# Scan of a bidirectional gated recurrence: filler weights' low parts by negative copy and accumulating DMA, one update per level for keys and queries, first decays copied by ScalarE

## The chip, the cores and the metric

The kernel runs on one core of a Trainium2 chip. The metric is the device time of one launch in microseconds (us), as the median of several runs. A profiled execution beside them gives the span from the first to the last instruction, and the records that are quoted below.

## What is computed

One layer of an encoder on a sequence of 1024 positions with 1024 channels, in float32. The part that this change is about is the two-way recurrence of one of its two token mixers, for 8 heads of 128 channels, in each direction:

```python
h = rmsnorm(x)
proj = h @ w_in                      # q, v, z_f, z_b, output gate, merge gates, ...
f = lb + (1 - lb) * sigmoid(z)       # decay per position and channel
k = (1 - lb) * sigmoid(-z)
S_t = diag(f_t) S_{t-1} + k_t v_t^T  # state, 128 x 128 per head
o_t = S_t^T q_t                      # forward and backward scan, added
```

The other mixer is a gated depthwise convolution. Both are merged by gates (sigmoid of the last columns of the projection), projected, and followed by a gated feed-forward part and a last norm.

## The kernel before

**Matmuls in float32.** A weight tile is split into a high part, rounded to the format that TensorE multiplies fast (fp32r), and a low part, the rest. `split` (L123) does so: ScalarE copies the raw page to the high part, and VectorE subtracts the high part from the raw page to get the low one. `mm3` (L147 to L149) then makes three matmuls per 128 rows: high weights with high inputs, high weights with low inputs, low weights with high inputs. The third is the first to read a low part.

**Jobs.** The projection's columns are computed 128 at a time by jobs (`std_job`). A job's `prep` loads the raw weights (`raw_w`, L134, 512 KB on SyncE's queue, two pages "wr") and splits them into two pages of four ("wp"). Its `run` issues 8 steps of six matmuls: 4 steps for each half of the sequence, each half ending with an `evac` that copies the result from the bank to a page "ev" (L720, L722) and stores it in DRAM. `run_jobs` prepares the next job when a job starts. `duo_job` runs two jobs, half by half.

**The scan stage.** After the convolution's pointwise jobs (tile "ch", pages of 512 elements), 22 columns of the projection are left, merge gates that nobody needs yet: 20 standard jobs and one `duo_job`. They are the stream `dense`, filler for TensorE while the scan runs. `dense.fill(1.3)` issues one step, sometimes two. The stream starts with `dense.fill(21)`, ahead of the first scan level.

The scan walks over 16 half-heads (8 heads, 2 halves of 512 positions). For each one:

- `scan_inputs` loads q and the gates' inputs z of both directions (L1060, L1063) and lets ScalarE compute the keys (k) and decays (f) from them.
- `scan_base` (L1078 on) builds products of decays inside blocks of 8 positions in the tile DE, a reciprocal, and from them the scaled queries Qh, qF and keys Kh, kG. It is a generator: the base of the next half-head is advanced by two steps at a time between the levels of the present one. `tt` (L1042) is its product on VectorE, `keys` (L1045) a scaled product.
- `scan_levels` takes four levels, with blocks of h = 8, 16, 32 and 64 positions. At h = 8 and 16 ScalarE copies the keys into a page A (L1160), and 16 small matmuls multiply A with the queries (L1162; bank "sc" at 8, bank "ob" at 16). At 32 and 64 the matmuls read keys and queries directly (L1188). Then one VectorE product each updates the keys (kG) and the queries (qF) by the blocks' decays tb, for the next level, and a small one merges tb.
- `scan_states` transposes the keys (L1245), copies them, multiplies them with the values (L1254) and chains the states on VectorE (Sf, L1260 and L1262; Sb, L1347).
- `scan_outputs`, spread over the next half-head, multiplies states and scores (L1295), normalises (a power on GpSimd, L509 and L510, and scaling on ScalarE, L1314), and transposes (L1321).

Between these steps `between(FILL)` issues filler steps, two base steps and one step of the pending outputs.

**Order.** TensorE's instructions run in the order in which the program issues them (`manual_schedule`). The other engines' order is laid out ahead of time by the framework's scheduler from the dependencies; every engine then runs its own list strictly in order, and waits on semaphores.

**DMA.** SyncE issues the ordinary ones. GpSimd issues those that add to their target (`accum_op`); before, only the pair jobs of other stages use them (L300).

Of the kernel before, what the change touches and what calls it, by code (L numbers as in the profile page):

```python
# [10 lines left out]
F32 = mybir.dt.float32  # L11
# [35 lines left out]
def tile_hybrid_encoder(  # L47
# [45 lines left out]
    def nm(s):  # L93
        uid[0] += 1
        return f"{s}_{uid[0]}"
# [6 lines left out]
    def page(pool, tag, bufs, dt=F32):  # L102
        return pool.tile([P, H], dt, tag=tag, name=nm(tag), bufs=bufs)
# [395 lines left out]
    def in_cols(c0):  # L499
        return w_cols(w_in, 0, ND, c0)  # L500
# [576 lines left out]
    def scan_base(ins):  # L1077


        q, f, kk, ks = ins  # L1080

        def two(t, *r):
            if len(r) == 1:
                return view(t, r[0], [[8, N2]])
            return view(t, r[0], [[r[1] - r[0], 2], [8, N2]])

        fv = lambda *r: two(f, *r)
        ed = lambda *r: two(DE, *r)
        D = D0


        V.tensor_copy(ed(2, D + 4), fv(3, 4))
# [24 lines left out]
        along = [[8, NB], [1, 8]]  # L1117
        for d in range(2):
            m0, st = ((0, 1), (7, -1))[d]
            whole = [[8, NB], [st, 8]]  # L1120
            tt(view(Qh, (1 - d) * H + m0, whole), view(q, m0, whole), view(DE, D + d * H, along))
            yield
            keys(
                view(Kh, d * H + m0, whole),
                view(kk, d * H + m0, whole),
                ks[:, d : d + 1],
                view(DE, d * H, along),
            )
            yield
        both = [[H, 2], [8, NB], [1, 8]]  # L1130
        tt(view(qF, 0, both), view(Qh, 0, both), view(fm, 0, [[NB, 2], [1, NB], [0, 8]]))
        yield
        tt(view(kG, 0, both), view(Kh, 0, both), view(DE, D + 7, [[H, 2], [8, NB], [0, 8]]))
        yield
        yield qF, kG, [(Qh[:, 1 - d, :], Kh[:, d, :]) for d in range(2)], tb

    def scan_levels(base, S_t, Tt):


        qF, kG, qk, tb = base  # L1140
# [16 lines left out]
        def level(b, h):  # L1157

            A_t = page(hp, "A", 2)
            A.copy(A_t.rearrange("p (b x e) -> p b x e", x=2, e=h), pairs(kG, h))  # L1160
            for at, g, o in each():
                T.matmul(  # L1162
                    b[g, o].rearrange("p (b x e) -> p b x e", x=2, e=h),
                    A_t[:, at : at + 32],
                    view(qF, at, [[2 * h, 16 // h], [H + h, 2], [1, h]]),
                    start=True,
                    stop=True,
                )
# [13 lines left out]
        def blocks(b, h):  # L1182

            for c in range(0, H, P):
                for s0 in range(0, P, h):
                    t0 = s0 ^ h
                    d = s0 // h % 2
                    T.matmul(  # L1188
                        b[s0 : s0 + h, c + t0 : c + t0 + h],
                        kG[:, d, c + s0 : c + s0 + h],  # L1190
                        qF[:, 1 - d, c + t0 : c + t0 + h],
                        start=True,
                        stop=True,
                    )
# [7 lines left out]
        for h in (8, 16, 32, 64):  # L1202
# [5 lines left out]
            else:  # L1208
# [1 line left out]
                    b = bank("sc")  # L1210
                    T.matmul(b, none[:, :P], none, start=True, stop=True)
                blocks(b, h)
            tt(pairs(kG, h), pairs(kG, h), view(tb, 1, [[2, n], [nb - 1, 2], [0, h]]))
            tt(pairs(qF, h), pairs(qF, h), view(tb, nb + 1, [[2, n], [nb - 1, 2], [0, h]]))
            if h < 64:
                tn = hp.tile([P, 3, NB], F32, tag="tb", name=nm("tb"), bufs=3)
                k = 3
# [17 lines left out]
                    A.copy(S_t[g : g + 32, :, g : g + 32], D_t[g : g + 32])  # L1235
            yield

    def scan_states(i, kG, v, Tt, Sf, Sb):

        half = i % 2  # L1240
        kTs = []
        for d in range(2):
            b = bank("tr")
            for c in range(4):
                T.transpose(b[:, c * P : (c + 1) * P], kG[:, d, c * P : (c + 1) * P], ident)  # L1245
            kT = page(hp, "kT", 2)
            A.copy(kT, b)
            kTs.append(kT)
            yield
# [27 lines left out]
    def scan_outputs(h, kept, Sf, Sb):  # L1277
# [3 lines left out]
        ss = cp.tile([P, 2, 4], F32, name=nm("oss"), tag="oss", bufs=2)  # L1281
        rs = cp.tile([P, 2, 4], F32, name=nm("ors"), tag="ors", bufs=2)
        for half in range(2):
            S_t, v, qF = kept[half]
            o = bank("ob")
            for c in range(4):
                sl = slice(c * P, (c + 1) * P)
                g = half * 4 + c
                terms = [(S_t[:, c, :], v[:, c, :])]
                if g > 0:  # L1290
                    terms.append((qF[:, 1, sl], Sf[half][:, c, :]))
                if g < 7:
                    terms.append((qF[:, 0, sl], Sb[half][:, c, :]))
                for n, (l, r) in enumerate(terms):
                    T.matmul(o[:, sl], l, r, start=(n == 0), stop=(n == len(terms) - 1))  # L1295
# [73 lines left out]
    for h in range(NH):  # L1369
# [4 lines left out]
        for half in range(2):  # L1374
# [13 lines left out]
            for n, _ in enumerate(scan_levels(base, S_t, Tt[:, half])):  # L1388
# [7 lines left out]
            qF, kG = base[0], base[1]  # L1396
            for _ in scan_states(i, kG, v, Tt, Sf, Sb):
                between(FILL)
            kept.append((S_t, v, qF))
            cur = ahead  # L1400
        pending = Stream(outputs(h, kept, Tt, Sf, Sb))

# [397 lines left out]
```

## Time and profile before

| what | value |
|---|---|
| median of 3 runs | 1792.36 us (1791.06 to 1793.42) |
| span of the profiled execution | 1788.8 us |
| granted TensorE clock, mean | 0.996 |
| TensorE matmul busy | 1733.0 us (97%) |
| TensorE weight load busy | 1416.7 us (79%) |
| VectorE busy | 1250.4 us (70%) |
| ScalarE busy | 775.0 us (43%) |
| GpSimd busy | 153.8 us (9%) |
| DMA, over the span | 155 GB/s, of queue q0 (GpSimd's) 32.51 MB |

The profile names engines PE (matmul), PEld (weight load), DVE (VectorE), ACT (ScalarE), POOL (GpSimd) and SP (SyncE). A group row gives the source line, engine, operation, output<-inputs by tile name, the shape, the count, and behind the bar the busy time, the mean duration in ns, and the idle time of the engine before them with what ended it. A wait row reads "who <- whom: us in total, times, longest". The scan stage is the stretch from 500 to 906 us. Matmuls are pipelined, so PE's busy time holds a little slack; its idle time is real.

### The profile page before, as it was taken

What the parts mean: (1) busy time and instruction counts of PE and PEld (TensorE: products, weight loads), DVE (VectorE), ACT (ScalarE), POOL (GpSimd) and SP (SyncE); (2) the same over time, 40 slices, a digit from 0 to 9 for tenths busy, and PEclk for the clock granted to TensorE, in tenths of its full rate; (3) what the DMA queues carried; (4) which work ended last, traced back from release to release, by engine and by line L of the source; (5) the groups of instructions that cost most, each with busy time, mean ns of one, the idle gap of its engine ahead of it and who ended that gap; (6) DMA issues with size and microseconds to landing.
All of it is one profiled execution on the core that took longest, in us unless ns stands there. A gap on an engine that the chain in (4) does not pass through costs nothing.

```text
span 1788.8 us, 27583 instructions
## 1 busy us (share of the span) xinstructions
PE 1733.0 (97%) x10632; PEld 1416.7 (79%) x10638; DVE 1250.4 (70%) x1884; ACT 775.0 (43%) x1490; POOL 153.8 (9%) x168
## 2 busy tenths in 40 slices
PE   8989999999999999999999999999999999999997
PEld 6878877888777777777778888878888888888885
DVE  5599999746569999999645557667667667544455
ACT  7344333334555566655442245344344344422123
POOL 2201111000000000000000002011111111000000
PEclk9999999999999999999999999999999999999999
DMA  8657887743663433333257665567667665534233
GB/s 285 216 151 187 185 185 185 199 150 126 199 214 101 125 119 119 119 119 101 90 180 219 200 201 177 153 142 159 151 144 158 142 151 133 161 103 126 79 91 135
DMA packets 317705, 276.41 MB, mean 155 GB/s; under 512 B 14462, under 2 KB 242566, under 8 KB 317574
## 3 DMA queue, kind: packets, MB, share of 16 engines
q1 hardware_dynamic: 276406, 242.15, 43.1%
q0 software_dynamic: 41168, 32.51, 12.6%
q8 instruction: 83, 1.36, 0.3%
q14 instruction: 48, 0.39, 0.1%
HBM read 185.73 MB, written 72.61 MB: 144 GB/s over the span
## 4 chain that ended last, share of the span: by engine, by line
PE 65%; DVE 19%; DMA 5%; issue 4%; ACT 4%; POOL 1%; SPq 0%; POOLq 0%; DVEq 0%; ACTq 0%
PE mm L147 16%; PE mm L148 16%; PE mm L149 16%; PE sc L147 3%; PE sc L149 3%; PE sc L148 3%; DVE acc L955 2%; DVE kG L1042 2%; DVE DE L1042 2%; DVE qF L1042 2%; DVE wp L123 2%; PE tr L147 1%; PE tr L149 1%; PE tr L148 1%; DVE DE L1098 1%
## 5 line engine op out<-in xcount | busy, mean ns | idle before, releaser
L147 PE MATMUL mm<-hx,wp 128*128 128x512 f32 x1128 | 454.8, 403 | 9.8 <-DVE ev L717 4.3
L149 PE MATMUL mm<-hx,wp 128*128 128x512 f32 x1128 | 441.7, 392 | 1.9 <-DVE wp L123 1.9
L148 PE MATMUL mm<-hx,wp 128*128 128x512 f32 x1128 | 441.4, 391 | 0.0
L123 ACT CAST wp<-wr 128x1024 fp32r<-128x1024 f32 (+2 forms) x179 | 167.0, 934 | 359.6 <-PE mm L148 271.5
L147 PEld LDWEIGHTS mm<-hx,wp 128*128 128x128 f32 x1128 | 212.5, 188 | 55.7 <-DVE ev L717 6.7
L123 DVE TENSOR_TENSOR wp<-wr,wp 128x1024 fp32r<-128x1024 f32 (+2 forms) x177 | 191.4, 1082 | 90.4 <-ACT wp L123 90.1
L149 PEld LDWEIGHTS mm<-hx,wp 128*128 128x128 f32 x1128 | 212.6, 188 | 49.3 <-DVE wp L123 3.2
L148 PEld LDWEIGHTS mm<-hx,wp 128*128 128x128 f32 x1128 | 212.9, 189 | 40.4 <-issue 0.2
L955 DVE SCALAR_TENSOR_TENSOR acc<-gl,v_b,acc 128x1024 f32<-128x1024 f32 x120 | 149.0, 1277 | 0.5
L1651 DVE TENSOR_TENSOR xr<-mm,xr 128x512 f32<-128x512 f32 x48 | 33.2, 691 | 73.1 <-PE mm L149 73.1
L367 ACT COPY su<-mm 128x512 f32<-128x512 f32 x78 | 45.2, 579 | 62.5 <-PE mm L149 61.5
L123 ACT CAST wq<-sw 128x1024 fp32r<-128x1024 f32 x39 | 41.0, 1051 | 64.4 <-issue 28.6
L1500 DVE SCALAR_TENSOR_TENSOR tm<-gp,v_a,tm 128x512 f32<-128x512 f32 x88 | 65.9, 749 | 2.0
L147 PE MATMUL mm<-hy,wp 128*128 128x512 f32 x156 | 61.5, 394 | 1.4 <-ACT su L367 1.4
L148 PE MATMUL mm<-hy,wp 128*128 128x512 f32 x156 | 61.1, 392 | 0.0
L147 PE MATMUL sc<-hy,wq 128*128 128x512 f32 x156 | 61.1, 392 | 0.0
L149 PE MATMUL sc<-hy,wq 128*128 128x512 f32 x156 | 61.1, 391 | 0.0
L147 PE MATMUL tr<-hx,wp 128*128 128x512 f32 x156 | 60.8, 390 | 0.0
L149 PE MATMUL tr<-hx,wp 128*128 128x512 f32 x156 | 60.7, 389 | 0.0
L148 PE MATMUL tr<-hx,wp 128*128 128x512 f32 x156 | 60.7, 389 | 0.0
L148 PE MATMUL sc<-hy,wq 128*128 128x512 f32 x156 | 60.7, 389 | 0.0
L149 PE MATMUL mm<-hy,wp 128*128 128x512 f32 x156 | 60.6, 389 | 0.0
(368 smaller groups left out, 3467.6 us busy)
## 6 DMA issues: line engine op xcount, KB each, us to landing
wr<-in_w_in_dram SPq DMA_DIRECT2D x56, 512.0 KB, 4.7
wr<-in_ffn_w_up_dram SPq DMA_DIRECT2D x24, 512.0 KB, 4.9
sw<-in_ffn_w_up_dram SPq DMA_DIRECT2D x44, 256.0 KB, 3.0
d_g<-ft SPq DMA_DIRECT2D x44, 256.0 KB, 2.7
sw<-in_ffn_w_up_dram POOLq DMA_DIRECT2D x20, 512.0 KB, 8.3
sw<-in_w_in_dram SPq DMA_DIRECT2D x34, 256.0 KB, 3.2
d_z<-ev SPq DMA_DIRECT2D x32, 256.0 KB, 3.1
zi<-d_z SPq DMA_DIRECT2D x32, 256.0 KB, 3.2
```

The lines of the kernel that those rows point to most:

```text
L123: parts = A.copy(hi, src), eng.tensor_tensor(lo, src, hi.bitcast(F32), op=ALU.subtract)
L147: T.matmul(acc, whi[:, k, :], ahi, start=first, stop=False, skip_group_check=again)
L148: T.matmul(acc, whi[:, k, :], alo, start=False, stop=False, skip_group_check=again)
L149: T.matmul(acc, wlo[:, k, :], ahi, start=False, stop=last, skip_group_check=again)
L367: A.copy(t, acc)
L955: V.scalar_tensor_tensor(acc, g[:, k : k + S], tap(k), acc, op0=ALU.mult, op1=ALU.add)
L1042: V.tensor_tensor(o, a, b, op=op)
L1098: V.reciprocal(ed(D, 7), ed(0, D + 7))
L1500: V.scalar_tensor_tensor(c, g[:, o + k : o + k + H], vec("fdw", k * NF + j), c, op0=ALU.mult, op1=ALU.add,)
L1651: V.tensor_tensor(xr[i][half], acc, xr[i][half], op=ALU.add)
```

## The change

1. **Filler weights.** The 20 standard jobs of `dense` become `dma_job`s. The high part is copied by ScalarE as before. The low part is now a second ScalarE copy, the high part times -1, onto which GpSimd's DMA adds the raw weights from DRAM. VectorE has no part in it. `fetch` loads the raw page of the next job one job ahead. The `duo_job` at the end stays as it was.
2. **One update per level.** kG and qF become planes of one tile KQ (planes 0 and 2 keys, 1 and 3 queries, three buffers), and the two products per level become one of 1024 elements per partition.
3. **First decays.** The copy into DE (L1092) goes from VectorE to ScalarE.
4. The pages for z go from three to two.

```diff
+    def dma_job(src, nk, acts, evac, fetch, after):
+        def prep():
+            raw = fetch(src)
+            if after is not None:
+                fetch(after)
+            hi, lo = w_page(nk), w_page(nk)
+            A.copy(hi, raw)
+            A.activation(lo, hi.bitcast(F32), AF.Copy, scale=-1.0)
+            G.dma_start(lo, src, accum_op=ALU.add)
+            return hi, lo
+
+        return prep, std_job(None, nk, acts, evac)[1]
...
-    rest_jobs = [std_job(in_cols(c), ND, h_std, e) for c, e in rest[:-2]]
+    srcs = [in_cols(c) for c, _ in rest[:-2]]
+    rest_jobs = [
+        dma_job(src, ND, h_std, e, fetch, after)
+        for src, (_, e), after in zip(srcs, rest, srcs[1:] + [None])
+    ]
...
-            z = page(hp, "zi", 3)
+            z = page(hp, "zi", 2)
...
-        V.tensor_copy(ed(2, D + 4), fv(3, 4))
+        A.copy(ed(2, D + 4), fv(3, 4))
...
-        qF = hp.tile([P, 2, H], F32, tag="qF", name=nm("qF"), bufs=3)
-        kG = hp.tile([P, 2, H], F32, tag="kG", name=nm("kG"), bufs=2)
+        KQ = hp.tile([P, 4, H], F32, tag="KQ", name=nm("KQ"), bufs=3)
...
-        def pairs(t, h):
-            return view(t, 0, [[2 * h, H // (2 * h)], [H + h, 2], [1, h]])
+        def pairs(h, n):
+            return view(KQ, 0, [[2 * h, n], [2 * H + h, 2], [1, h]])
...
-            A.copy(A_t.rearrange("p (b x e) -> p b x e", x=2, e=h), pairs(kG, h))
+            A.copy(A_t.rearrange("p (b x e) -> p b x e", x=2, e=h), pairs(h, H // (2 * h)))
...
-            tt(pairs(kG, h), pairs(kG, h), view(tb, 1, [[2, n], [nb - 1, 2], [0, h]]))
-            tt(pairs(qF, h), pairs(qF, h), view(tb, nb + 1, [[2, n], [nb - 1, 2], [0, h]]))
+            tt(pairs(h, nb), pairs(h, nb), view(tb, 1, [[2, nb], [nb - 1, 2], [0, h]]))
```

The other edits only read keys and queries from their planes of KQ.

More of the change, by code (lines that the diff above doesn't have):

```diff
@@ L1016, in tile_hybrid_encoder, with fetch @@
     rest = todo[2 * NPAIRS :]
-    rest_jobs = [std_job(in_cols(c), ND, h_std, e) for c, e in rest[:-2]]
+    fetched = {}
+    def fetch(src):
+        at = src.offset
+        if at not in fetched:
+            fetched[at] = raw_w(src, ND)
+        return fetched[at]
+    srcs = [in_cols(c) for c, _ in rest[:-2]]
[3 more added lines that the diff above has]
+    ]
     (c0, e0), (c1, e1) = rest[-2:]
@@ L1129, in scan_base @@
             yield
-        both = [[H, 2], [8, NB], [1, 8]]
-        tt(view(qF, 0, both), view(Qh, 0, both), view(fm, 0, [[NB, 2], [1, NB], [0, 8]]))
+        both, apart = [[H, 2], [8, NB], [1, 8]], [[2 * H, 2], [8, NB], [1, 8]]
+        tt(view(KQ, H, apart), view(Qh, 0, both), view(fm, 0, [[NB, 2], [1, NB], [0, 8]]))
         yield
-        tt(view(kG, 0, both), view(Kh, 0, both), view(DE, D + 7, [[H, 2], [8, NB], [0, 8]]))
+        tt(view(KQ, 0, apart), view(Kh, 0, both), view(DE, D + 7, [[H, 2], [8, NB], [0, 8]]))
         yield
-        yield qF, kG, [(Qh[:, 1 - d, :], Kh[:, d, :]) for d in range(2)], tb
+        yield KQ, [(Qh[:, 1 - d, :], Kh[:, d, :]) for d in range(2)], tb
     def scan_levels(base, S_t, Tt):
-        qF, kG, qk, tb = base
-        def pairs(t, h):
-            return view(t, 0, [[2 * h, H // (2 * h)], [H + h, 2], [1, h]])
+        KQ, qk, tb = base
+        def pairs(h, n):
+            return view(KQ, 0, [[2 * h, n], [2 * H + h, 2], [1, h]])
         def near(t):
@@ L1164, in level @@
                     A_t[:, at : at + 32],
-                    view(qF, at, [[2 * h, 16 // h], [H + h, 2], [1, h]]),
+                    view(KQ, H + at, [[2 * h, 16 // h], [2 * H + h, 2], [1, h]]),
                     start=True,
@@ L1189, in blocks @@
                         b[s0 : s0 + h, c + t0 : c + t0 + h],
-                        kG[:, d, c + s0 : c + s0 + h],
-                        qF[:, 1 - d, c + t0 : c + t0 + h],
+                        KQ[:, 2 * d, c + s0 : c + s0 + h],
+                        KQ[:, 3 - 2 * d, c + t0 : c + t0 + h],
                         start=True,
@@ L1236, in scan_levels, with scan_states @@
             yield
-    def scan_states(i, kG, v, Tt, Sf, Sb):
+    def scan_states(i, KQ, v, Tt, Sf, Sb):
         half = i % 2
@@ L1244, in scan_states @@
             for c in range(4):
[L1245 removed]
+                T.transpose(b[:, c * P : (c + 1) * P], KQ[:, 2 * d, c * P : (c + 1) * P], ident)
             kT = page(hp, "kT", 2)
@@ L1283, in scan_outputs @@
         for half in range(2):
-            S_t, v, qF = kept[half]
+            S_t, v, KQ = kept[half]
             o = bank("ob")
@@ L1290, in scan_outputs @@
                 if g > 0:
-                    terms.append((qF[:, 1, sl], Sf[half][:, c, :]))
+                    terms.append((KQ[:, 3, sl], Sf[half][:, c, :]))
                 if g < 7:
-                    terms.append((qF[:, 0, sl], Sb[half][:, c, :]))
+                    terms.append((KQ[:, 1, sl], Sb[half][:, c, :]))
                 for n, (l, r) in enumerate(terms):
@@ L1395, in tile_hybrid_encoder @@
                 between(FILL)
-            qF, kG = base[0], base[1]
-            for _ in scan_states(i, kG, v, Tt, Sf, Sb):
+            KQ = base[0]
+            for _ in scan_states(i, KQ, v, Tt, Sf, Sb):
                 between(FILL)
-            kept.append((S_t, v, qF))
+            kept.append((S_t, v, KQ))
             cur = ahead
```

## The prediction, made before the changed kernel was run

> **What bounds the kernel now.** I began with the engines' busy time by window, because the change touches one stage alone: the scan with its dense filler jobs, 500 to 906 us on the profile's axis.
>
> ```profile
> 600.00:700.00 100.00, 94.48 (x1243) 77.23 (x1245) 92.70 (x193) 57.13 (x141) 4.48 (x4) 1.00 0.39 123
> ...
> 500.00:906.00 406.00, 384.88 (x4694) 315.42 (x4698) 346.20 (x700) 230.75 (x560) 14.44 (x17) 1.00 0.37 118
> ```
>
> The columns are the window and its length, then busy time of TensorE, its weight load, VectorE, ScalarE and GpSimd, the granted clock, the DMA share and GB/s. In the middle TensorE works 94.5% of the time and VectorE 92.7%. So both are nearly full, the clock is whole, and all that can be won here is TensorE's idle time: 406.0 - 384.9 = 21.1 us, 1.2% of the span. The waits of TensorE in this window tell what that idle time is.
>
> ```profile
> PE ob L1162 <- DVE qF L1042: 6.0, 7, 1.5
> PE tr L1245 <- DVE kG L1042: 4.9, 7, 1.8
> PE sc L1188 <- DVE qF L1042: 3.8, 7, 1.2
> PE ob L1295 <- DVE Sb L1347: 1.4, 1, 1.4
> PE ob L1295 <- DVE D L1230: 1.1, 1, 1.1
> ```
>
> Each row gives the total, the number of waits and the longest. They add to 17.2 us, all on VectorE, mostly on the per-level updates of keys (kG) and queries (qF). The change's target is thus the right one. Whether it hits depends on two things: how late an update starts, and how long the chain is from one level's matmuls to the next's.
>
> **What leaves VectorE.**
>
> ```profile
> L1042 DVE TENSOR_TENSOR qF<-qF,tb 128x512 f32<-128x512 f32 x64 | 43.8, 684 | 0.4 <-PE sc L1162 0.4
> L1042 DVE TENSOR_TENSOR kG<-kG,tb 128x512 f32<-128x512 f32 x64 | 43.6, 682 | 3.5 <-PE sc L1188 2.9 <-ACT A L1160 0.4
> ...
> L123 DVE TENSOR_TENSOR wp<-wr,wp 128x1024 fp32r<-128x1024 f32 x22 | 26.9, 1222 | 12.7 <-ACT wp L123 12.7
> ...
> L1042 DVE TENSOR_TENSOR kG<-Kh,DE 128x1024 f32<-128x1024 f32 x16 | 19.5, 1219 | 0.1
> ...
> L1092 DVE COPY DE<-f 128x256 f32<-128x256 f32 x16 | 6.7, 418 | 0.0
> ```
>
> Twenty subtractions for low parts at 1.222 us: 24.4 us. Sixty-four pairs of 512 elements become one of 1024: 0.684 + 0.682 - 1.219 (the price of the x16 row with 1024 elements) = 0.147 us each, 9.4 us. Sixteen copies at 0.418: 6.7 us. Together 40.5 us of 346, so VectorE falls from 92% to some 82% in the middle.
>
> **What goes to ScalarE** is twenty negative copies of 1024 elements and sixteen copies of 256.
>
> ```profile
> L123 ACT CAST wp<-wr 128x1024 fp32r<-128x1024 f32 x21 | 21.9, 1044 | 18.2 <-PE mm L148 16.0 <-DMA wr<-in_w_in_dram 2.1
> ...
> L1160 ACT COPY A<-kG 128x512 f32<-128x512 f32 x32 | 19.7, 616 | 20.9 <-DVE kG L1042 20.8
> ```
>
> 20 x 1.044 = 20.9 us, and 16 x 0.4 (between nothing and the 0.616 of 512 elements; nearest VectorE's own 0.418) = 6.4 us. ScalarE goes from 231 to 258 of 406 us, 64%; it does not become a bound, and I price its load at nothing beside the chain below. The first decays are read only after the reciprocal and several products behind it on VectorE, which cover the copy.
>
> **The accumulating DMA.** No 512 KB accumulation runs in this stage before, but 31 run elsewhere.
>
> ```profile
> sw<-in_ffn_w_up_dram POOLq DMA_DIRECT2D x20, 512.0 KB, 8.3
> ...
> sw<-in_w_in_dram POOLq DMA_DIRECT2D x11, 512.0 KB, 8.8
> ```
>
> The last number is the median from issue to landing. A single one, issued at 1164.7, is the fast end:
>
> ```profile
> sw<-in_ffn_w_up_dram POOLq DMA_DIRECT2D x1, 512.0 KB, 6.6
> ```
>
> So a low part is there 1.04 + 8.3 = 9.3 us after its high part, where the subtraction took 1.22. In the steady stage that is hidden. Preparation of job n+1 starts with job n, and the high parts tell how far apart jobs are:
>
> ```profile
> L123 ACT CAST wp<-wr x18: 1032/1044/1053, 537.7 to 882.2; 128x1024 fp32r<-128x1024 f32 x18
> ```
>
> (882.2 - 537.7) / 17 = 20.3 us, against 1.04 + 1.04 + 8.3 = 10.4: some 10 us to spare. Extra traffic (10.5 MB) meets a DMA share of 0.37. GpSimd was busy 14.4 us; behind a waiting issue stands only the output scale's power, which is needed some steps later. Two pages for the gates' inputs instead of three still leave a whole half-head between a page's last reader and its next load. All of this I take as nothing.
>
> **The first job is not hidden.** It is prepared while the last pointwise job runs. Its page comes free only then, so its work starts 3.3 us before TensorE reads the low part:
>
> ```profile
> 497.75 1.05 ACT L123 CAST wp<-wr 128x1024 fp32r<-128x1024 f32 x1 [1.68 <-PE mm L148]
> ```
> ```profile
> 500.80 0.53 POOL L1036 MEMSET none<- 128x512 bf16 x1 [0.76 <-PE mm L149]
> 500.80 0.39 PE L148 MATMUL mm<-hx,wp 128*128 128x512 f32 x1
> ...
> 501.03 0.40 PE L149 MATMUL mm<-hx,wp 128*128 128x512 f32 x1
> ```
>
> Columns: start, duration, engine. The third matmul (L149, 501.03) reads the low part. Afterwards the negative copy can run from 498.80 to 499.84. The DMA is issued then, or at about 501.4 if GpSimd's queue has the memsets first. It lands at 499.8 + 6.6 = 506.4 at the earliest, at 501.4 + 8.8 = 510.2 at the latest. TensorE's order is written by hand, so nothing else fills: it stands for 5.4 to 9.2 us. I take 499.8 + 8.3 = 508.1, **+7 us**. The second job is prepared during the first and has the stall besides; the third has one job of 48 matmuls, 0.23 us from one start to the next (500.80 to 501.03), some 11 us, against 10.4: nothing, at most 2 us.
>
> The Trainium skill, "DMA: Bandwidth & Descriptors", section "Anatomy of one DMA — SWDGE (gpsimd) path", fits a GpSimd-issued DMA as 2.0 us plus bytes over 436 GB/s; for 512 KB that is an estimate of 3.2 us, and the first job's stall by it would be 2 us. The 31 accumulations of this trace took 8.3 and 8.8 us in the median, so I go by them.
>
> **The chain from level 8 to level 16 grows.** Until now the keys' update waits only for ScalarE's copy A of the keys, and can run a level ahead of TensorE. The merged one also writes the queries, so it waits for the level's matmuls. Behind it come the next copy A, and then the next matmuls. Beside it TensorE has one filler step of six matmuls, sometimes two. Two passages, the second with transposes besides:
>
> ```profile
> 758.40 0.45 PE L1162 MATMUL sc<-qF,A 128*32 128x32 f32 x30
> ...
> 759.19 1.22 DVE L123 TENSOR_TENSOR wp<-wr,wp 128x1024 fp32r<-128x1024 f32 x1
> ...
> 761.16 0.46 PE L1162 MATMUL ob<-qF,A 128*32 128x32 f32 x32 [0.74 <-DVE qF L1042]
> ```
> ```profile
> 643.14 0.45 PE L1162 MATMUL sc<-qF,A 128*32 128x32 f32 x30
> ...
> 644.07 0.68 DVE L1042 TENSOR_TENSOR kG<-kG,tb 128x512 f32<-128x512 f32 x1
> ...
> 645.55 0.46 PE L1162 MATMUL ob<-qF,A 128*32 128x32 f32 x32
> ```
>
> In the first, level 8 ends at 758.85 and TensorE is back at 761.16 - 0.74 = 760.42. Without the subtraction VectorE could start at 759.2: + 1.22 + 0.62 (copy A) + 0.1 for hand-overs = 761.1, idle 0.7 us as before. In the second, VectorE is free at 644.07: + 1.94 = 646.0, where nothing was lost: +0.45. Per half-head I take +0.3 (between 0, if each update starts at once, and 0.75, if it starts 0.6 us later still), 16 times: **+5 us** (0 to +12). From level 16 on, an update of 1.22 stands where two of 0.68 stood back to back, or, at the transposes, where 0.68 alone did.
>
> **Relief elsewhere.** The other VectorE waits are 4.9 + 3.8 + 1.4 + 1.1 = 11.2 us. They come from VectorE's queue, which loses a tenth of its work, but the transposes' link grows by 0.54. I take half gone, **-5 us** (-11 to +2); the first passage's waits fall in the first job's stall and are counted here.
>
> **Sum:** 7 + 5 - 5 = +7 us. The profiled execution has a span of 1788.8 us and the median of the runs is 1792.36, 3.6 above, for what lies around it. The span becomes 1795.8, the time **1799.4 us**, +0.4%. A difference of 0.2%, 3.6 us, is about what a measurement tells from none.
>
> **Rivals.**
> - *The relief wins (faster).* The place is level 16. If the scheduler, with a lighter VectorE queue, starts each merged update as its matmuls end, the chain is 1.94 us against a cover of 1.57 (760.42 - 758.85) and 1.96 (645.55 - 643.59): some 0.3 us, 5 us in all, and the other 11 us go. The stage's idle is then near 9; with 5.4 for the first job 14.4, against 21.1: -7, **1785 us**. It turns at an idle of 14 us beside the first job's stall. For it: 17.2 of 21 us wait for VectorE. Against: in both passages VectorE was in other work when the level ended. Chance 0.22.
> - *The low parts come late in many jobs (much slower).* ScalarE is in order; it waits 16.0 us for pages in the row above, and the negative copy, GpSimd's issue and the landing follow in series. If half of twenty jobs lose 1.5 us more, +15: **1814 us**. Against: 10 us to spare. Chance 0.13.
> - *It washes out.* The first job's stall gives VectorE a lead that lasts, the stall is near 5.4 and the level chain costs nothing net: +5.4 - 5 = 0, **1792 us**. Chance 0.13.
>
> The forecast has 0.52, its own range 1796 to 1806. Eight in ten: 1785 (half of the first rival below) to 1812 (most of the second above). Faster by over 0.2%: 0.22; within: 0.13; slower: 0.52 + 0.13 = 0.65.
>
> **What would show it.** Right: an idle of 5 to 9 us of TensorE before the first filler job's third matmul, released by the accumulating DMA; a larger sum for ob L1162, now released by ScalarE's copy A; less for L1188 and L1295; VectorE near 306 us in the stage; no DMA wait in later jobs. Wrong: no stall at the first job (the DMA lands in under 2 us, or is issued earlier), or ob L1162 under 6 us, which means the merged updates start at once; and a wait for low parts in many jobs, which means the spare 10 us were not there.

## The result, and the profile after

| what | before | after |
|---|---|---|
| median | 1792.89 us (1791.06 to 1794.90, 4 runs) | 1821.13 us (1820.34 to 1822.68, 4 runs) |
| span of the profiled execution | 1788.8 us | 1820.9 us |
| granted TensorE clock, mean | 0.996 | 0.988 |

The ratio is 1.0152, with a 95% interval of 1.0134 to 1.017: slower, by 28 us where the forecast had 7, and above the top of the range, 1812. The direction came out, the size did not.

The place was the foreseen one. Each filler job has 48 matmuls in both kernels, so the first matmul of the same job can be set side by side in the two traces: job 0 starts 3.2 us later than before, job 1 15.4 later, job 2 15.4, and the matmuls behind the last job 31.5 later; at the end of the span it is 32.1. The 3.2 us arise ahead of the change, where both kernels have the same instructions. Two things are left: 12.2 us at the first job, and some 16 spread over the rest of the scan.

The windows of the changed kernel, in the columns of the prediction's first fence:

```profile
600.00:700.00 100.00, 93.24 (x1159) 76.03 (x1158) 78.47 (x150) 62.87 (x153) 10.13 (x8) 0.98 0.51 129
...
500.00:906.00 406.00, 369.39 (x4391) 299.96 (x4391) 305.81 (x577) 250.84 (x565) 45.98 (x38) 0.97 0.57 139
```

VectorE was relieved as planned, from 92.7 to 78.5 us in the middle hundred; a part of that fall is that less of the scan lies in these hundred. For TensorE put 1159 matmuls through them instead of 1243, and its clock is no longer whole. TensorE's waits in the stage, which now lasts to 945 us:

```profile
PE ob L1188 <- ACT A L1186: 17.0, 13, 3.3
PE mm L149 <- DMA wp<-in_w_in_dram: 10.2, 2, 9.3
PE tr L1270 <- DVE KQ L1069: 2.8, 7, 0.7
PE tr L1346 <- ACT tm L1339: 2.1, 1, 2.1
PE sc L1279 <- ACT kT L1272: 1.5, 3, 0.9
PE sc L1188 <- ACT A L1186: 1.5, 2, 1.2
PE ob L1320 <- DVE Sb L1372: 1.4, 1, 1.4
PE sc L1214 <- DVE KQ L1069: 1.3, 1, 1.3
```

Lines have moved: L1188 is the level matmul of blocks 8 and 16 (L1162 before), L1186 the copy A, L1214 the blocks of 32 and 64 (L1188 before), L1270 the key transposes, L1069 the product, L1119 the copy of the first decays. Two rows are new at the top, 17.0 us ahead of level 16 and 10.2 us for low parts (9.3 in the first job, 0.9 in the third). The row of the transposes fell from 4.9 to 2.8 and that of the blocks from 3.8 to 1.3.

**The first job**, in the timeline (start, duration, engine, and in brackets the idle time and its releaser):

```profile
502.47 1.06 ACT L276 ACTIVATE wp<-wp 128x1024 fp32r<-128x1024 f32 x1
...
503.83 1.62 POOL L277 DMA_DIRECT2D wp<-in_w_in_dram  x1 [44.74 <-PE mm L148]
```
```profile
513.66 0.79 PE L149 MATMUL mm<-hx,wp 128*128 128x512 f32 x1 [9.26 <-DMA wp<-in_w_in_dram]
514.25 0.63 PE L147 MATMUL mm<-hx,wp 128*128 128x512 f32 x1
514.68 0.63 PE L148 MATMUL mm<-hx,wp 128*128 128x512 f32 x1
```

The negative copy ends at 503.53, the DMA is issued at 503.83, and the matmul that reads the low part starts at 513.66. TensorE stood for 9.26 us. Then the matmuls come 0.43 us apart (514.25 to 514.68) instead of 0.23. The windows of this stretch show why, and what the DMAs did meanwhile (the last three columns are the granted clock, the DMA share and GB/s):

```profile
503.00:514.00 11.00, 1.74 (x8) 1.13 (x7) 0.00 (x0) 4.93 (x6) 4.36 (x6) 0.78 1.07 257
```
```profile
513.00:520.00 7.00, 6.34 (x16) 4.99 (x17) 1.34 (x2) 3.08 (x5) 0.00 (x0) 0.54 1.24 257
```

Half the clock is granted until 519.4 us; 13 matmuls at 0.20 us too much are 2.6 us. Stall and slow clock are 12 us together. The landing, in the rows of DMA issues (KB, median us to landing), first of all twenty and then of this one alone:

```profile
wp<-in_w_in_dram POOLq DMA_DIRECT2D x20, 512.0 KB, 8.4
```
```profile
wp<-in_w_in_dram POOLq DMA_DIRECT2D x1, 512.0 KB, 9.8
```

The median came as priced, 8.3. This first one took 9.8, in a stretch where the DMA engines are full (share 1.07, against 0.57 over the stage): the loads of the scan's first inputs run with it.

**A passage from level 8 to level 16.** VectorE, ScalarE and TensorE in one timeline of the changed kernel:

```profile
784.40 1.74 DVE L1125 RECIPROCAL DE<-DE 128x256 f32<-128x256 f32 x1
...
785.42 0.45 PE L1188 MATMUL sc<-KQ,A 128*32 128x32 f32 x30
...
786.82 1.20 DVE L1069 TENSOR_TENSOR KQ<-KQ,tb 128x1024 f32<-128x1024 f32 x1
...
788.05 0.62 ACT L1186 COPY A<-KQ 128x512 f32<-128x512 f32 x1 [0.69 <-DVE KQ L1069]
...
788.72 0.46 PE L1188 MATMUL ob<-KQ,A 128*32 128x32 f32 x32 [1.29 <-ACT A L1186]
```

Level 8 ends at 785.87. VectorE is inside the next half-head's reciprocal until 786.14, then does three small products, and starts the merged update at 786.82. Copy A follows it, and TensorE, which had six filler matmuls, waits 1.29 us. The update's own chain (1.20 + 0.03 + 0.62 + 0.05 = 1.90 us) is the predicted one; the 0.95 us ahead of it come from what stands in VectorE's queue. The reciprocal had not been there: in the trace of before it never lies between the end of level 8 or 16 and the queries' update, in 32 passages. In the changed kernel it lies there 10 times (8 behind level 8, 2 behind level 16). That was the surprise, and the third theory below.

### The profile page after: what moved, and what is told of

It reads as the page before. It is cut to its first block, busy times and chain, and to the rows that moved or that the text cites. A ratio compares the mean times of both kernels' runs of the same rounds, so it can differ in the third digit from the quotient of the medians.

```text
span 1820.9 us, 27583 instructions
## 1 busy us (share of the span) xinstructions
PE 1746.3 (96%) x10638; PEld 1423.2 (78%) x10638; DVE 1221.0 (67%) x1784; ACT 804.6 (44%) x1526; POOL 185.8 (10%) x188
## 4 chain that ended last, share of the span: by engine, by line
PE 45%; DMA 3%; DVE 3%; issue 2%; ACT 2%; POOL 1%; SPq 0%; POOLq 0%; ACTq 0%; DVEq 0%
PE mm L147 12%; PE mm L148 12%; PE mm L149 12%; PE sc L149 2%; PE sc L147 2%; PE sc L148 2%; DMA sw<-in_ffn_w_up_dram 2%; DMA wr<-wr 1%; PE tr L147 1%; PE tr L148 1%; PE tr L149 1%; PE ob L1320 1%; DVE KQ L1069 1%; DMA wr<-sw 0%; DVE Sb L1372 0%
## 5 line engine op out<-in xcount | busy, mean ns | idle before, releaser
L149 PE MATMUL mm<-hx,wp 128*128 128x512 f32 x1128 | 445.5, 395 | 11.6 <-DMA wp<-in_w_in_dram 10.2
L123 ACT CAST wp<-wr 128x1024 fp32r<-128x1024 f32 (+2 forms) x159 | 146.2, 920 | 357.0 <-PE mm L148 257.0
L123 DVE TENSOR_TENSOR wp<-wr,wp 128x1024 fp32r<-128x1024 f32 (+2 forms) x157 | 168.0, 1070 | 89.9 <-ACT wp L123 89.6
L1069 DVE TENSOR_TENSOR KQ<-KQ,tb 128x1024 f32<-128x1024 f32 x64 | 77.9, 1217 | 9.7 <-PE sc L1188 6.1
L315 POOL DMA_DIRECT2D wr<-sw x31 | 27.7, 894 | 375.7 <-DVE wp L123 232.5
L147 PE MATMUL mm<-hy,wp 128*128 128x512 f32 x156 | 61.6, 395 | 2.1 <-ACT su L382 2.1
L148 PE MATMUL mm<-hy,wp 128*128 128x512 f32 x156 | 61.1, 392 | 0.0
L147 PE MATMUL sc<-hy,wq 128*128 128x512 f32 x156 | 61.1, 392 | 0.0
L149 PE MATMUL sc<-hy,wq 128*128 128x512 f32 x156 | 61.0, 391 | 0.0
```

Source lines behind the costliest of these rows:

```text
L123: parts = A.copy(hi, src), eng.tensor_tensor(lo, src, hi.bitcast(F32), op=ALU.subtract)
L147: T.matmul(acc, whi[:, k, :], ahi, start=first, stop=False, skip_group_check=again)
L148: T.matmul(acc, whi[:, k, :], alo, start=False, stop=False, skip_group_check=again)
L149: T.matmul(acc, wlo[:, k, :], ahi, start=False, stop=last, skip_group_check=again)
L315: G.dma_start(o, a, accum_op=ALU.add)
L1069: V.tensor_tensor(o, a, b, op=op)
```

## The experiments

Three theories for the 28 us: **(1)** the first filler job's low part comes late; **(2)** the merged update lengthens the way from level 8 to 16; **(3)** the copy of the first decays on ScalarE, priced at nothing, costs by what it does to VectorE's order. The rival to (1) was the prediction's, low parts late in many jobs; the rival to (2) that the shared tile, not the merging, costs; the rival to (3) that the copy costs as load on ScalarE. All ratios are to the kernel before, run beside each experiment, with 95% intervals; 0.2% is 3.6 us.

### Each part alone

**The accumulating DMA alone** (dma_only): before, with `dma_job` and `fetch` as in the change.

```diff
-    rest_jobs = [std_job(in_cols(c), ND, h_std, e) for c, e in rest[:-2]]
+    rest_jobs = [dma_job(src, ND, h_std, e, fetch, after) for ...]
```

> Only the filler weights' low parts change; updates of keys and queries stay two per level, and the first decays stay on VectorE. Theory: the first job's 12 us minus some relief for VectorE: 1798 to 1806 us, with no DMA wait after the second job. Rival (the accumulating DMAs cost throughout): 1815 us or more.

Measured: 1803.31 us beside 1795.93, ratio 1.0047 (1.003 to 1.0064). TensorE waits 11.1 us for low parts, in the first and the third job only (10.3 and 0.8), and job 1 starts 14 us late; up to 4 us of that come back later. The prediction's rival of low parts late in many jobs has no wait to show, here or in the changed kernel.

**The merged update alone** (merge_only): before, with KQ and one product per level, two z pages, the decays' copy left on VectorE.

```diff
-            tt(pairs(kG, h), pairs(kG, h), view(tb, 1, [[2, n], [nb - 1, 2], [0, h]]))
-            tt(pairs(qF, h), pairs(qF, h), view(tb, nb + 1, [[2, n], [nb - 1, 2], [0, h]]))
+            tt(pairs(h, nb), pairs(h, nb), view(tb, 1, [[2, nb], [nb - 1, 2], [0, h]]))
```

> Only the merged update (tile KQ, two pages for z); low parts and first decays stay on VectorE. Theory: the copy A for level 16 now waits for level 8's matmuls, so TensorE waits there about 17 us in all against 6.8: 1800 to 1810 us. Rival (one instruction instead of two is what relieves VectorE, the waits at level 16 come from elsewhere): 1793 us or less.

Measured: 1805.67 beside 1795.93, 1.005 (1.0032 to 1.0067). The two largest waits of TensorE in it:

```profile
PE ob L1176 <- ACT A L1174: 13.4, 10, 1.8
PE tr L1258 <- DVE KQ L1057: 7.5, 7, 2.3
```

Against 6.0 and 4.9 before, that is 10.0 us more, but other rows fell: all of TensorE's waits in the stage together rose by 6 us, and the time by 9.7. The rest fits the granted clock, which is half in four stretches of 3.4 us of this scan and whole in the scan of before. In 10 passages of 16 the update and the copy behind it outlast TensorE's filler; and the keys for the transposes, now in the same product as the queries, come later.

**The decays' copy alone** (decays_only): before, with one line changed.

```diff
-        V.tensor_copy(ed(2, D + 4), fv(3, 4))
+        A.copy(ed(2, D + 4), fv(3, 4))
```

> Only the first decays are copied by ScalarE. Theory: VectorE's products into DE wait for that copy in its queue (9.4 us of such waits in the changed kernel's profile), so it gives no gain and may cost: ratio 1.000 to 1.004, with DE waiting for ScalarE's DE. Rival (16 copies off VectorE are a relief): ratio 0.996 to 0.999.

Measured: 1808.60 beside 1794.66, 1.0091 (1.0076 to 1.0106). Both theories had this too small: the line that moves 6.7 us of work off VectorE is the costliest single part, +14 us by the medians and 16 by the ratio. It isn't a direct wait: VectorE waits for the copy once, 0.3 us. First TensorE's waits in this kernel, then a stretch of VectorE with the matmuls behind it:

```profile
PE ob L1162 <- DVE qF L1042: 12.5, 10, 3.0
PE sc L1188 <- DVE qF L1042: 5.5, 8, 1.4
PE sc L1162 <- ACT A L1160: 4.7, 5, 2.1
```
```profile
752.24 0.46 PE L1162 MATMUL ob<-qF,A 128*32 128x32 f32 x32
...
752.93 1.74 DVE L1098 RECIPROCAL DE<-DE 128x256 f32<-128x256 f32 x1
...
755.16 0.67 DVE L1042 TENSOR_TENSOR qF<-qF,tb 128x512 f32<-128x512 f32 x1
...
755.88 0.46 PE L1188 MATMUL sc<-qF,kG 128*32 128x32 f32 x32 [1.36 <-DVE qF L1042]
```

Level 16 ends at 752.70, and the queries' update, 0.67 us long, starts 2.46 us later, because the next half-head's reciprocal stands ahead of it in VectorE's list. It lies so in 8 of the 32 passages (4 behind level 8, 4 behind level 16). From the end of a level to the next level's matmuls TensorE idles 11.8 us in these 8 passages and 7.4 in the other 24; before, it was 8.9 in all 32.

### Parts taken out of the changed kernel

**The first filler job prepared as before** (first_std):

```diff
+    rest_jobs[0] = std_job(srcs[0], ND, h_std, rest[0][1])
```

> Theory: the changed kernel's 28 us are (a) the first filler job's wait for its low part, 9.3 us idle and about 2.6 us of half-clock matmuls behind it, (b) the longer chain from level 8 to level 16, some 10 us of TensorE waits, and (c) half-clock stretches that these pauses bring on. With the first filler job prepared by VectorE as before, (a) goes: about 1809 us (1805 to 1812). Rival: accumulating DMAs and their traffic slow the whole stage, and the first wait is made up later anyway: 1816 us or more.

Measured: 1819.03 beside 1795.93, 1.0124 (1.0099 to 1.0149). A miss: the wait went to the second job (4.3 us, one wait) and level 16 rose to 19.2 us, with the reciprocal in the way 11 times. One job as cover isn't enough, since the second job's page is prepared in the same stretch.

**The same, with two products per level in the KQ tile** (two_updates):

```diff
-            tt(pairs(h, nb), pairs(h, nb), view(tb, 1, [[2, nb], [nb - 1, 2], [0, h]]))
+            tt(part(0, h, n), part(0, h, n), view(tb, 1, [[2, n], [nb - 1, 2], [0, h]]))
+            tt(part(H, h, n), part(H, h, n), view(tb, nb + 1, [[2, n], [nb - 1, 2], [0, h]]))
```

> The changed kernel with the first filler job prepared by VectorE and with two updates per level, keys and then queries, in the one tile KQ. Theory: both known costs go and VectorE's relief is left: 1785 to 1795 us, TensorE's wait at level 16 at or under 7 us. Rival (the accumulating DMAs cost throughout): as with the merged update and the same first job, within 3 us of it.

Measured: 1810.51 beside 1795.93, 1.0087 (1.0065 to 1.0109). Without the merge, and with the first job covered, it is still 15 us above the kernel before; level 16 waits 12.2 us, and the reciprocal is in the way 10 times. What was left of the change here was the decays' copy and the second job's wait; this miss led to decays_only.

**The decays' copy given back to VectorE** (undo_decays): the changed kernel, with one line the other way.

```diff
-        A.copy(ed(2, D + 4), fv(3, 4))
+        V.tensor_copy(ed(2, D + 4), fv(3, 4))
```

> The changed kernel with the first decays copied by VectorE again. Theory: VectorE's waits for ScalarE's copy delay the merged updates (up to 3 us late at level 16 in three passages); without them the wait at level 16 falls from 17 to about 13 us, as with the merged update alone, and the time to 1814 to 1818 us. Rival (ScalarE's load by negative copies makes copy A late): no change, 1820 to 1823 us.

Measured: 1811.02 beside 1794.66, 1.0102 (1.0086 to 1.0119), some 9 us less than the changed kernel and below the 1814 to 1818 us of the theory. Level 16 waits 9.7 us instead of 17.0, and the reciprocal is in the way in no passage. A second thing goes with the copy here. In the changed kernel VectorE did wait for it, ahead of the reciprocal:

```profile
DVE DE L1069 <- ACT DE L1119: 9.4, 7, 3.6
```

This is the base's second product, DE<-f,DE. It reads and writes other columns of DE than the copy does, and still it waits.

**The accumulating DMA from the fourth job on** (dma_from_fourth): dma_only, with three standard jobs first.

```diff
+    rest_jobs[:3] = [
+        std_job(s, ND, h_std, e) for s, (_, e) in zip(srcs[:3], rest)
+    ]
```

> The accumulating DMA alone, from the fourth filler job on; the first three are prepared by VectorE, updates and first decays are as before the change. Theory: the DMA's only price is the first job's wait and its half clock; from there on it relieved VectorE (dma_only gained about 5 us between the first and the last level 8): 4 to 6 us under the kernel before, ratio 0.997 to 0.998, no DMA wait of TensorE. Rival (that relief came from VectorE's lead during the first wait, not from the DMA): ratio 0.999 to 1.002.

Measured: 1790.48 beside 1794.66, 0.9977 (0.9966 to 0.9988). This is faster than both kernels. TensorE's three largest waits:

```profile
PE tr L1275 <- DVE kG L1072: 6.4, 8, 1.7
PE ob L1192 <- DVE qF L1072: 2.8, 7, 0.5
PE sc L1218 <- DVE qF L1072: 2.7, 4, 1.3
```

No low part is waited for, so the whole price of the DMA was at the start: 1.0047 against 0.9977 is 0.7%, 12.6 us. And level 16 fell from 6.0 to 2.8: VectorE's relief is real, and 4 us is what it buys. It came at level 16; the transposes' row rose, from 4.9 to 6.4.

**The merge on top of that** (merge_from_fourth): the changed kernel with these three standard jobs and the decays on VectorE.

```diff
-        A.copy(ed(2, D + 4), fv(3, 4))
+        V.tensor_copy(ed(2, D + 4), fv(3, 4))
...
+    rest_jobs[:3] = [
+        std_job(s, ND, h_std, e) for s, (_, e) in zip(srcs[:3], rest)
+    ]
```

> The changed kernel without its two dearest parts: first three filler jobs prepared by VectorE, first decays copied by VectorE; the merged update and the accumulating DMA stay. Theory: the first job's 13 us go from the 1811 us of the version that undid the decays alone, TensorE waits some 10 us at level 16: ratio 1.000 to 1.004 to the kernel before. Rival (the merged update costs less than the chain says): ratio 0.998 or less, with the DMA alone at 0.9977.

Measured: 1799.19 beside 1795.68, 1.0024 (1.0011 to 1.0037). Against dma_from_fourth the merge costs 0.47%, 8.4 us, nearly what it cost alone, and the relief of VectorE doesn't cure it:

```profile
PE ob L1191 <- ACT A L1189: 10.0, 10, 1.8
PE tr L1273 <- DVE KQ L1072: 4.9, 8, 1.9
```

**The same with more filler behind level 8** (merge_cover), and less elsewhere:

```diff
-                between(FILL)
+                between(2.1 if n == 0 else 7 / 6)
...
-                between(FILL)
+                between(7 / 6)
```

> As the version with merged update, first three filler jobs by VectorE and decays by VectorE, and the filler steps are shared out otherwise: 2.1 behind level 8 and 7/6 behind each of the six other steps, 9.1 in all as before. Theory: the merged update's only fault is that its chain is longer than TensorE's cover of 1.6 us at level 16; with a cover near 3 us the wait there falls under 3 us: 3 to 8 us under the same version with even steps. Rival (the wait moves to the steps that lose cover, above all to the key transposes): within 3 us of it, with L1270's wait up by what level 16's is down.

Measured: 1804.18 beside 1795.68, 1.0054 (1.0036 to 1.0073). The cover does what theory (2) says at level 16, but the time rose, by 5 us against merge_from_fourth. The wait moved to the steps that lost cover, as the rival has it, though hardly to the key transposes that it names first (4.9 to 5.3). The largest waits:

```profile
PE ob L1323 <- DVE tb L1072: 9.3, 7, 2.1
PE tr L1273 <- DVE KQ L1072: 5.3, 6, 1.6
PE sc L1217 <- DVE KQ L1072: 3.0, 7, 0.9
PE ob L1191 <- ACT A L1189: 3.0, 5, 1.5
```

Level 16 fell from 10.0 to 3.0 us, but the output matmuls (L1323) rose from 2.9 to 9.3 behind the same VectorE queue. The first low part that comes by DMA, the fourth job's, is late again by 1.4 us. The filler is a fixed sum; moved, it uncovers another wait.

### What exactly costs

**One tile, two products** (one_tile_two_updates): merge_only with the level's product split into two again, as in two_updates.

```diff
-            tt(pairs(h, nb), pairs(h, nb), view(tb, 1, [[2, nb], [nb - 1, 2], [0, h]]))
+            tt(part(0, h, n), part(0, h, n), view(tb, 1, [[2, n], [nb - 1, 2], [0, h]]))
+            tt(part(H, h, n), part(H, h, n), view(tb, nb + 1, [[2, n], [nb - 1, 2], [0, h]]))
```

> The kernel before with keys and queries as planes of one tile KQ (two pages for z), still updated by two products. Theory: the copy A of the keys waits for the queries' product too, because both are in one tile with interleaved ranges, and so the chain over level 8's matmuls is there without any merging: TensorE's wait at level 16 is 10 us or more, ratio 1.003 to 1.007, as with the merged update alone. Rival (the dependency is the merged instruction's alone): ratio 0.999 to 1.001, wait at level 16 about 7 us.

Measured: 1793.34 beside 1795.68, 0.9991 (0.9979 to 1.0003). The shared tile and two z pages cost nothing; the merging does. Level 16 does wait for copy A here (9.1 us), as the theory has it, but the transposes wait 1.8 us where they waited 4.9 before, and the blocks 1.7 instead of 3.8.

**The decays' copy on ScalarE, behind the reciprocal** (decays_late, on the kernel before; after_decays_late, on the changed one):

```diff
-        V.tensor_copy(ed(2, D + 4), fv(3, 4))
...
         V.reciprocal(ed(D, 7), ed(0, D + 7))
         yield
 
+        A.copy(ed(2, D + 4), fv(3, 4))
```

> The kernel before with the first decays copied by ScalarE behind the reciprocal instead of ahead of the first product. Theory: with the copy in front, VectorE's second product waits for it, though it reads other columns, and the reciprocal (1.76 us) is laid between level 8's matmuls and the queries' update; placed late it holds up nothing: ratio 0.997 to 1.001, reciprocal never in that place. Rival (ScalarE's 0.7 us per copy is the cost, wherever it stands): ratio 1.006 to 1.010 as with the copy in front.

> The changed kernel with ScalarE's copy of the first decays issued behind the reciprocal instead of ahead of it. Theory (the copy costs by its place: VectorE's second product waits for it, and the reciprocal slips between a level's matmuls and the merged update): the gain is that of giving the copy back to VectorE, about 10 us: 1807 to 1813 us, ratio 1.008 to 1.011, and VectorE's 9.4 us of waits for the copy are gone. Rival (the copy costs by its load on ScalarE, whose copies A come later): the gain is under 3 us: 1818 us or more, ratio 1.013 or more.

Measured: 1792.68 beside 1795.68, 0.9985 (0.997 to 1.0); and 1808.89 beside 1793.58, 1.0096 (1.008 to 1.0113). The same copy, on the same engine, of the same length, costs nothing from the later place, and in the changed kernel the move gives back 0.56%, 10 us. The reciprocal is in the way in no passage of either. The expectation that VectorE's 9.4 us of waits for the copy would be gone was a miss: another product waits for it now. Its row, of VectorE's waits in after_decays_late:

```profile
DVE fm L1069 <- ACT DE L1127: 5.4, 7, 1.6
```

So ScalarE's load is not what costs. VectorE's waiting for the copy isn't needed for the cost either, as decays_only has 0.3 us of it and the highest price. In the changed kernel the later place both frees the updates of the reciprocal and cuts these waits from 9.4 to 5.4 us; the runs do not divide the 10 us between the two. Of the kernels traced, the four that issue the copy on ScalarE ahead of the first product have the reciprocal in the way (8, 10, 11 and 10 times of 32), and the other twelve never. That the planner moves the reciprocal because it expects the copy later is argued from this, not shown: its plan isn't in the trace.

**Both harmless parts together** (dma4_decays_late): dma_from_fourth with the copy on ScalarE behind the reciprocal.

```diff
-        V.tensor_copy(ed(2, D + 4), fv(3, 4))
...
+        A.copy(ed(2, D + 4), fv(3, 4))
```

> The kernel before with the accumulating DMA from the fourth filler job on, and ScalarE's copy of the first decays behind the reciprocal. Theory (both only lighten VectorE, 21 us of subtractions and 6.7 us of copies, and no wait replaces them): the two ratios multiply, 0.9977 x 0.9985 = 0.996, some 1788 us beside 1795, between 0.9945 and 0.998. Rival (VectorE's slack is already enough with the first part, so the copy adds nothing, or ScalarE's copies A come later): 0.9977 or higher, up to 1.000.

Measured: 1789.99 beside 1793.58, 0.9984 (0.9975 to 0.9993): faster than before, and not apart from dma_from_fourth's 0.9977. Another 6 us off VectorE (326.9 us busy from 500 to 906, against 332.8) bought nothing more; the waits of TensorE are those of dma_from_fourth within 0.6 us a row, save one of the outputs.

**The subtractions on GpSimd** (pool_lo): before, the filler's low parts subtracted by GpSimd.

```diff
+            return split(w_page(nk), w_page(nk), raw, G)
```

> The kernel before with the low parts of the 20 filler jobs subtracted by GpSimd instead of VectorE, no DMA. Theory: VectorE is relieved as with the DMA, and the first job has to wait at most 1 to 2 us (a subtraction of 512 elements on GpSimd took 1.29 us, so some 2.6 for 1024): ratio 0.996 to 0.999. Rival (GpSimd and VectorE hinder each other at their operands): VectorE's products grow, ratio 1.000 or more.

Measured: 1816.42 beside 1794.66, 1.0135 (1.0119 to 1.0152). Its groups of GpSimd and of VectorE in the stage:

```profile
L123 POOL TENSOR_TENSOR wp<-wr,wp 128x1024 fp32r<-128x1024 f32 x20 | 63.7, 3185 | 228.3 <-ACT wp L123 218.2 <-PE ob L1170 10.0
```
```profile
L1050 DVE TENSOR_TENSOR qF<-qF,tb 128x512 f32<-128x512 f32 x62 | 48.2, 778 | 1.2 <-PE sc L1170 1.0
```

VectorE lost 24 us of subtractions, and its queries' updates went from 684 to 778 ns in the mean. The mean hides two kinds. Of all 64, the 56 that overlap no subtraction of GpSimd took 684 ns as before (709 at most), and of the 8 that do overlap one, four took 1.07 to 2.84 us. One of them, with the subtraction beside it:

```profile
732.91 2.42 POOL L123 TENSOR_TENSOR wp<-wr,wp 128x1024 fp32r<-128x1024 f32 x1 [10.74 <-ACT wp L123]
```
```profile
733.04 2.84 DVE L1050 TENSOR_TENSOR qF<-qF,tb 128x512 f32<-128x512 f32 x1
```

It ends 0.55 us after the subtraction. Level 16 waits 16.9 us in this kernel. Here the DMA earns its place: it is the one way tried that takes the low parts off VectorE without slowing VectorE's other products.

## Why the prediction was wrong in size

The ladder from the best run to the changed kernel, each rung one part, in ratios: dma_from_fourth 0.9977 (relief, -4 us); the merge, 1.0024 (+8); the first three jobs through the DMA, 1.0102 (+14); the decays' copy ahead of VectorE's products, 1.0152 (+9). They add to the changed kernel's +27 by construction, as each rung starts where the last one ends; what the runs give is the size of each, with an uncertainty of some 3 us. In another order the sizes differ: alone, the copy cost 14 to 16.

- **First job's stall, +7 (5.4 to 9.2): right in mechanism, too small.** The stall was 9.3 us in the changed kernel and 10.3 in dma_only. By its steps: the negative copy ended at 503.53, 0.7 us ahead of the third matmul's turn (504.02 + 0.23 = 504.25) where 1.2 was foreseen, mostly since another ScalarE copy came between the two; the issue came 0.3 us later; and this one DMA took 9.8 us, 1.0 more than the upper bound and 1.5 more than was taken. That is 0.5 + 0.3 + 1.5 on top of 7.1, or 9.4, and the matmul did start 513.66 - 504.25 = 9.4 us late. And the prediction stopped at the stall. TensorE's clock fell to half behind it, which cost 2.6 us more. In time the jobs of the start cost 14 us (the ladder), twice the term.
- **Level 8 to 16, +5 (0 to 12): in its range, the mechanism right in part.** Measured +8.4 in time for the merge, and the wait did pass to copy A. But one_tile_two_updates has 9.1 us of that wait without any merging and is no slower than before. What merge_only has above it is 4.3 us at level 16 and 5.7 at the transposes (7.5 against 1.8), whose link the prediction put under relief.
- **Relief, -5: near in size, by luck; the place was another.** It measured -4.2 us (dma_from_fourth). The prediction looked for it in the transposes, the blocks and the outputs, and not at level 16. In dma_from_fourth level 16 gave 3.2 us and the blocks 1.1, while the transposes' row rose by 1.5 and the outputs' rows by 2.0 (1.4 + 1.1 before, 1.8 + 1.4 + 1.3 there).
- **The copy of the first decays on ScalarE, priced at nothing: the step that failed.** The prediction had ScalarE's load "at nothing", and the decays "read only after the reciprocal and several products behind it on VectorE, which cover the copy". That is an argument about data, and it misses two things. The base's second product, ahead of the reciprocal, waited for the copy although it reads none of it: 9.4 us in the changed kernel, 0.3 in decays_only. And an engine's order is laid out anew from the dependencies, while the prediction took VectorE's order as given and moved an instruction that stands first in that chain. The price was 9 to 10 us in the changed kernel and 14 to 16 alone, where it came through a 1.74 us reciprocal ahead of a 0.67 us update; in the changed kernel the reciprocal stood ahead of a 1.20 us update, and the waits came on top. The copy itself was also dearer than its upper bound of 0.616 us, here in ScalarE's groups:

```profile
L1119 ACT COPY DE<-f 128x256 f32<-128x256 f32 x16 | 11.3, 704 | 0.0
```

- **VectorE's 40.5 us off: right as a sum of durations.** Over the scan the subtractions' row fell from 28.1 to 3.7 us, the updates' from 87.4 to 77.9, and 6.7 of copies went. That the busy time of the two windows fell by 346.2 - 305.8 = 40.4 us is chance: the second window lacks 123 instructions where the change takes out 100. Over the whole run VectorE's busy time fell by 29.3 us (1250.4 to 1221.0), since neighbouring instructions overlap and busy time counts the overlap once. It decided nothing: in this stage TensorE waited for when VectorE did a thing, not for how much it had to do.
- **The rivals.** The relief didn't win, as level 16 stayed over 9 us with every merged update but one kernel's. The late low parts stayed with the first and the third job, where the prediction allowed up to 2 us and 0.9 came. It did not wash out either, with a stall of 9.3 us instead of 5.4. The prediction had no rival in which the order of VectorE's list gets worse, and that is why the range ended 9 us short.

What stays open: how much of the later loss is the clock's and how much the waits' (bounds are below), and why the profiled execution was already 3.2 us later ahead of the stage. There the two kernels' instructions are the same; 1.2 of the 3.2 us arise at 311 to 318 us, where the granted clock is half for 6.8 us instead of 3.4.

## What to carry to other kernels

When an operation moves to another engine in a kernel whose order a planner lays out, price the place it gets and what moves with it, not only its duration: look for the longest instruction of the next stage (here a 1.74 us reciprocal) and ask whether it can land between a producer and its waiting reader. An accumulating DMA takes work off a full engine cheaply, but its landing must be covered from its first use on: here three jobs prepared the old way turned 1.0047 into 0.9977. Merging two updates saves instructions and joins their waits; where one half could run ahead, the merged one can't.

## What the hardware showed that was not expected

- **A stall costs more than its length.** Behind the 9.3 us without matmuls the matmuls came 0.43 us apart instead of 0.23, until 519.4 us. The granted clock of the changed kernel is half in four stretches of the scan, from 509.1 for 10.2 us, 591.1 for 6.8, 642.3 and 939.2 for 3.4 each; in the kernel before it is whole from 314 to 1167 us. They are all multiples of 3.4 us. The Trainium skill, "TensorE: Matmul & The Clock Gate", section "Part 1: The HAM clock gate (the "warmup" mystery)", says that the clock drops to 4/8 after an idle window of about 3.4 us and that these windows run freely. The trace agrees on the 0.5 granted and the pieces of 3.4 us. It does not bear out that such a window has to be idle throughout: in the 3.4 us ahead of the three later dips TensorE stood still for 1.7, 1.8 and 2.1 us, while its longest later wait, 3.3 us up to 838.5 us, brought none. The next two rows hold the same filler matmuls, from the first one to the last, in the kernel before and in the changed one:

```profile
500.58:920.10 419.52, 396.30 (x4742) 324.39 (x4747) 352.00 (x707) 238.43 (x577) 16.23 (x18) 1.00 0.38 118
```
```profile
503.78:951.70 447.92, 407.18 (x4749) 330.71 (x4748) 323.53 (x608) 267.41 (x612) 47.82 (x40) 0.97 0.55 135
```

Of the 28.4 us that the changed kernel needs more here, 17.5 are idle time of TensorE (40.7 against 23.2) and 10.9 are more busy time for the same matmuls. Without the first job's 9.3 and 2.6, some 8 us of each are left. The three later dips, 13.7 us at half clock, can lose 6.8 of that at most.
- **A product on GpSimd holds up VectorE's.** In pool_lo GpSimd took 3185 ns in the mean for the subtraction that VectorE does in 1222 (16 of the 20 took 2.4 to 2.9 us, the others 4.5 to 8.6), and four of VectorE's queries' updates beside one took up to 2.84 us instead of 0.68. The Trainium skill, "SBUF — State Buffer", section "Who interferes with whom", describes an exclusive lock between these two engines, where the second to issue waits out the first. The pair of rows above agrees: VectorE's update, begun 0.13 us behind the subtraction, ended 0.55 us after it. The four other overlapping updates, 673 to 692 ns, were not held up.
- **The copy of the first decays was slower on ScalarE.** Its 256 elements, which lie eight apart, took 704 ns there and 418 on VectorE, while ScalarE's copy A of 512 elements took 616. Whether the spacing is the reason, no run tells.
